# Paged scoring: POOL's scaling and subtraction of the scores issued behind the low half of the next group, and the high products first in the first pair

## The chip, the cores and the metric

The kernel runs on one core of one Trainium2 chip. The metric is the device time of one execution in microseconds (us). A difference of 0.2% (3.7 us) is about what a measurement of this kernel can tell from none.

## The reference, cut to what matters

The reference is one layer of a decoder for two groups of requests: a prompt of 1024 tokens, and 8 sample requests of 4 tokens each, whose past of 4096 tokens lies in a paged cache. The change touches the attention of the sample requests over this cache:

```python
def one(args):                                  # for each of the 8 requests
    pages, q1, c1, pe1 = args
    c_all = jnp.concatenate([pool_ckv[pages].reshape(PAST_LEN, KV_LORA), c1], axis=0)
    pe_all = jnp.concatenate([pool_kpe[pages].reshape(PAST_LEN, QK_ROPE), pe1], axis=0)
    k, v = mla_keys_values(c_all, pe_all, k_pos, w_uk, w_uv, g_qk_k)   # k is RMS-normalised per head
    return masked_attend(q1, k, v, q_pos, k_pos)                       # softmax(q k / sqrt(96)) v
```

For each of 32 pages of 128 tokens the kernel needs the scores of 8 heads x 4 queries, and for each token and head the squared length of its key, by which the scores are scaled before the softmax.

## The kernel before, in words

The program runs through a projection, the prompt's attention, the stage on the pages, the memory's keys and values, the output projection, the memory attention and the FFN. On the page stage, `phase2b` writes the order out by hand: 128 steps n, one for each pair of pages, 16 steps for one request (called batch b here); `at(n, pos, f)` puts a piece of work at a position of a step, and `run` issues it there. The order in which PE (TensorE), ACT (ScalarE), DVE (VectorE) and POOL (GpSimd) get their instructions is the order of issue (`manual_schedule`), up to step 128. SP's queue of loads in that stretch, and the compute engines behind it, are ordered by a scheduler.

Two steps share a quad of four pages:

- `quad_load` loads it transposed (`cT`) and plain (`ck`), three quads ahead. `quad_prep`, at an even step n, lets ACT round `cT` into the high part `ch` (L1362, two instructions, one for each half k of the 256 latent dimensions); at position (n+1, -2) it issues the low part `cl = cT - ch` (L1366): half k=0 on POOL, half k=1 on DVE. PE uses them from step n+2 on. `quad_rot` (L1351 to L1353) gives POOL three operations on the rope keys of two quads ahead, at the end of each odd step.
- `pair_score` is PE's work of a step. For each of two pages e it multiplies the page (stationary) with a 288-column and a 256-column piece of the weights and queries, each product split into three: high x high, high x low, low x high, for k=0 and then k=1. `mm3` (L185) issues these six in a row, so the third product of a group needs POOL's half of `cl` and the sixth DVE's. ACT squares what comes out (L1403, L1406), DVE adds the scores to `S` (L1405) and sums the squares into `ss` (L1409).

When the first 24 pages of a batch are scored, `batch_softmax` begins its pieces r: DVE turns `ss` into reciprocal roots (r 0 to 2); POOL scales 24 pages of `S` by them (r=3, L1427, at step 14 of the batch, position 3); DVE takes the maximum (r=4, L1430, at 15, position 0); the last 8 pages follow (r 5 to 8); PE, DVE and ACT bring the maximum to all partitions (r 9 to 11: ACT's copy `bc`, L1469); POOL subtracts it from `S` (L1470, also in r=11, at step 20, position 2); ACT takes the exponential (r=12, L1472, at 21, position 3). Then `quad_pv` (L1481) multiplies the weights with the values, `batch_out` (L1489 to L1499) copies and divides, `batch_close` (L1505, L1506) folds. Since the next batch is being scored meanwhile, POOL has these two operations between its `cl` halves.

Behind step 128 the generator `mem_kv` takes the keys and values of the memory: ACT makes `mh` (L204) and DVE `ml` (L207) out of the memory in eight pieces, PE multiplies them (L1549) into a PSUM tile `b` with two buffers, ACT reads each as `kr` and `sq` (L1555, L1557). The last steps of the page stage and the pieces of the last batch's softmax are issued between its parts.

Of the kernel before, what the change touches and what calls it, by code (L numbers as in the profile page):

```python
# [9 lines left out]
ALU = mybir.AluOpType  # L10
# [3 lines left out]
P = 128  # L14
NP_, NS, NT = 1024, 32, 1056
NB, ND = 8, 4
# [138 lines left out]
class Net:  # L155
# [987 lines left out]
    def phase2b(self):  # L1143
        nc, tc, I = self.nc, self.tc, self.I
        pa = self.pa3 = self.open("p3a", side="right")
        pt, px, p = self.open("p3t"), self.open("mx"), self.open("p3")
        self.mx0 = [self.t(px, [P, 8, 384], FR, f"mx0{x}") for x in "hl"]
        wk0 = [self.t(px, [P, 8, P], FR, f"wk0{x}") for x in "hl"]
        ppt, pp = self.open("ps3t", space=PSUM), self.open("ps3", space=PSUM)
# [13 lines left out]
        last = NB * 16  # L1163
        st, ev, late = {}, {}, []

        def at(n, pos, f, *a):
            ev.setdefault((n, pos), []).append(lambda: f(*a))
# [27 lines left out]
        for b in range(NB):  # L1195
            n = b * 16
            at(n - 10, 0, lambda b: st.__setitem__(b, self.batch_open(p, b)), b)
            at(n - 8, 2, lambda b: self.batch_enter(st[b], b), b)
            for r, (k, pos) in enumerate(((12, 0), (13, 0), (14, 0), (14, 3), (15, 0), (16, 0), (17, 0), (17, 3), (18, 2), (19, 2), (20, 0), (20, 2), (21, 3))):
                f = lambda b=b, r=r: self.batch_softmax(p, ppt, st[b], r, b == NB - 1)  # L1200
                if n + k <= last:
                    at(n + k, pos, f)
                else:
                    late.append(f)
            n += 16 + LAG + 15
            tail = (
                lambda b=b: self.batch_out(pt, st[b], 0),
                lambda b=b: self.batch_out(pt, st[b], 1, ppt, b == NB - 1),
                lambda b=b: self.batch_close(pt, ppt, b, st.pop(b)),
            )  # L1210
            for k, pos, f in ((0, 3, tail[0]), (2, 2, tail[1]), (3 if b == NB - 2 else 4, 3, tail[2])):
                if b < NB - 1:
                    at(n + k, pos, f)
# [48 lines left out]
        with tc.manual_schedule(engines={E.SP}):  # L1262
            self.close("ps3")
            for x in ("p3a", "p3c", "sq", "sm"):
                self.close(x)
            self.wr = self.open("wr", bufs=3, side="right")
            self.wp = self.open("w", bufs=3, side="right")
            mem = self.mem_kv(raws, wk0)
            for f in late[:3]:
                f()  # L1270
            for _ in range(6):
                next(mem)
            steps(last + 1, last + 7)
            for f in late[3:]:
                f()
            for _ in range(6):
                next(mem)
            steps(last + 7, last + 16 + LAG)
            for _ in mem:
                pass  # L1280
# [105 lines left out]
    def pair_score(self, p, pp, n, d, s, rope):  # L1386
        nc = self.nc
        b, g0 = n // 16, n % 16 * 2
        off, sc = (0, 0) if b % 2 == 0 else (32, 256)
        n0 = 32 - off  # L1390

        ps = self.t(pp, [P, 2, 512], F32, "s", 2)
        pt = self.t(pp, [P, 512], F32, "s2", 2)
        k2 = [[[d[x][:, k, g0 % 4 + e].rearrange("p j t -> p (j t)") for x in "hl"] for k in range(2)] for e in range(2)]
        w = lambda a, z: [(self.w2h[:, k, a:z], self.w2l[:, k, a:z]) for k in range(2)]
        if rope:
            rope = self.quad_rope(ps[:, 0, 320:448], *rope)
        for e in range(2):
            self.mm3(ps[:, e, :288], k2[e], w(off, off + 288))
        for e in range(2):  # L1400
            self.mm3(pt[:, e * 256 : e * 256 + 256], k2[e], w(320, 576))
        sq = self.t(p, [P, 2, 2, 256], F32, "sq", 2)
        nc.scalar.activation(sq[:, 0], ps[:, :, n0 : n0 + 256], AF.Square)  # L1403
        S = s["S"][:, g0 : g0 + 2]
        nc.vector.tensor_tensor(S, ps[:, :, sc : sc + 32], S, ALU.add)  # L1405
        nc.scalar.activation(sq[:, 1], pt.rearrange("p (e d) -> p e d", e=2), AF.Square)  # L1406
        if rope:
            yield rope
        yield lambda: nc.vector.tensor_reduce(  # L1409
            s["ss"][:, g0 : g0 + 2].rearrange("p e (z h) -> p z e h", z=2), sq.rearrange("p z e (h d) -> p z e h d", h=4), AX.X, ALU.add  # L1410
        )

    def batch_softmax(self, p, pp, s, r, final):

        nc = self.nc
        S, ss = s["S"], s["ss"]

        def norms(g0, g1, e=nc.vector):
            x = ss[:, g0:g1]
            e.tensor_tensor(x, x, s["kss"][:, g0:g1].unsqueeze(2).broadcast_to([P, g1 - g0, 8]), ALU.add)  # L1420
            sf = x.rearrange("p g h -> p (g h)")
            return self.rsqrt_steps(p, sf, sf, 1.0 / 96, e)

        def scale(e, g0, g1):
            n = (g1 - g0) * 8
            x = S[:, g0:g1].rearrange("p g (h t) -> p (g h) t", h=8)
            e.tensor_tensor(x, x, ss[:, g0:g1].rearrange("p g h -> p (g h)").unsqueeze(2).broadcast_to([P, n, 4]), ALU.mult)  # L1427

        def peak(z, g0, g1):
            nc.vector.tensor_reduce(s["m"][:, z], S[:, g0:g1].rearrange("p g m -> p m g"), AX.X, ALU.max)  # L1430

        if r == 0:
            s["it"] = norms(0, 24)
            next(s["it"])
        elif r == 1:
            next(s["it"])
        elif r == 2:
            for _ in s["it"]:
                pass
        elif r == 3:  # L1440
            scale(nc.gpsimd, 0, 24)
        elif r == 4:
            s["m"] = self.t(p, [P, 2, 32], F32, "mx", 2)
            peak(0, 0, 24)
        elif r == 5:
            s["it"] = norms(24, 32, nc.gpsimd if final else nc.vector)
            next(s["it"])
        elif r == 6:
            next(s["it"])
        elif r == 7:  # L1450
            for _ in s["it"]:
                pass
        elif r == 8:
            scale(nc.vector, 24, 32)
            peak(1, 24, 33)
            nc.vector.tensor_tensor(s["m"][:, 0], s["m"][:, 0], s["m"][:, 1], ALU.max)
        elif r == 9:
            tp = s["tp"] = self.t(pp, [P, 512], F32, "m", 1)
            nc.tensor.transpose(tp[:32, :P], s["m"][:, 0], self.ident)
        elif r == 10:  # L1460
            mm = self.t(p, [32, 1], F32, "mm", 2)
            nc.vector.tensor_reduce(mm, s["tp"][:32, :P], AX.X, ALU.max)
            s["dg"] = self.t(p, [32, 32], F32, "dg", 2)
            nc.vector.tensor_scalar(s["dg"], self.ident[:32, :32], mm, None, ALU.mult)
        elif r == 11:
            bc = self.t(pp, [P, 512], F32, "m", 1)[:, :32]
            self.spread = nc.tensor.matmul(bc, self.ones[:32], s["dg"], start=True, stop=True)
            s["bc"] = self.t(p, [P, 32], F32, "bc", 2)
            nc.scalar.copy(s["bc"], bc)  # L1469
            (nc.vector if final else nc.gpsimd).tensor_tensor(S, S, s["bc"].unsqueeze(1).broadcast_to([P, 33, 32]), ALU.subtract)  # L1470
        else:
            self.exp = nc.scalar.activation(S, S, AF.Exp, scale=SCALE)  # L1472

    def quad_pv(self, pp, Q, d, s):

        nc, S, q = self.nc, s["S"], Q % 8
        if q == 0:
            s["o"] = self.t(pp, [P, 512], F32, "o", 1)[:, :257]
            nc.tensor.matmul(s["o"][:32], S[:, 32], self.cn[:, :257], start=True, stop=False)
        for j in (1, 2, 3, 0):  # L1480
            nc.tensor.matmul(  # L1481
                s["o"][j * 32 : j * 32 + 32], S[:, q * 4 + j], d["ck"][:, j, :257], start=q == 0 and j > 0, stop=q == 7
            )
# [973 lines left out]
```

## Time and profile before

| | |
|---|---|
| Median of 3 runs | 1832.22 us (1831.4 to 1832.39) |
| The profiled execution, its own time | 1835.1 us |
| Its span, first to last instruction | 1833.4 us |
| Mean granted TensorE clock | 0.996 |
| Page stage, 400 to 858 us of the span: PE busy | 451.71 of 458 us |
| same stretch: DVE, ACT, POOL busy | 337.00, 267.50, 212.84 us |

Rows of the timeline read: start in the span, duration (of a group, if it ends in x2 or more: from the first start to the last end), engine, line, operation, output tile <- input tiles, size, count, and in brackets the idle time before it with what ended it. PE's records are longer than the distance between two starts, as products overlap; where PE is dense, the start-to-start distance is the cost of a product.

### The profile page before, as it was taken

What the parts mean: (1) busy time and instruction counts of PE and PEld (TensorE: products, weight loads), DVE (VectorE), ACT (ScalarE), POOL (GpSimd) and SP (SyncE); (2) the same over time, 40 slices, a digit from 0 to 9 for tenths busy, and PEclk for the clock granted to TensorE, in tenths of its full rate; (3) what the DMA queues carried; (4) which work ended last, traced back from release to release, by engine and by line L of the source; (5) the groups of instructions that cost most, each with busy time, mean ns of one, the idle gap of its engine ahead of it and who ended that gap; (6) DMA issues with size and microseconds to landing.
All of it is one profiled execution on the core that took longest, in us unless ns stands there. A gap on an engine that the chain in (4) does not pass through costs nothing.

```text
span 1833.4 us, 39288 instructions
## 1 busy us (share of the span) xinstructions
PE 1806.0 (99%) x14226; PEld 1702.6 (93%) x14226; DVE 1352.0 (74%) x2807; ACT 921.9 (50%) x1910; POOL 695.7 (38%) x845
## 2 busy tenths in 40 slices
PE   9999999999999999999999999999999999999999
PEld 8999777769999999998899979999999999999999
DVE  7854767757778766787645666998888888888664
ACT  7435676766655555556433556533333333444442
POOL 1021555624445444453033110377667776400000
PEclk9999999999999999999999999999999999999999
DMA  8102363558866666654555156222222222495242
GB/s 321 47 19 72 104 196 116 162 186 237 220 179 192 193 177 186 181 169 138 174 168 185 49 180 188 81 82 76 96 75 71 81 72 82 143 332 163 79 153 77
DMA packets 153187, 261.18 MB, mean 142 GB/s; under 512 B 20897, under 2 KB 97538, under 8 KB 152994
## 3 DMA queue, kind: packets, MB, share of 16 engines
q1 hardware_dynamic: 152130, 257.63, 45.4%
q8 instruction: 112, 1.84, 0.4%
q10 hardware_dynamic: 864, 1.05, 0.2%
q14 instruction: 81, 0.66, 0.1%
HBM read 212.79 MB, written 45.82 MB: 141 GB/s over the span
## 4 chain that ended last, share of the span: by engine, by line
PE 73%; issue 4%; DVE 4%; DMA 2%; SPq 2%; ACT 2%; POOL 1%; DVEq 0%; POOLq 0%; ACTq 0%
PE s L185 15%; PE d L185 12%; PE b L185 8%; PE F L185 7%; PE X L185 7%; PE E L185 7%; PE A L185 3%; PE y L185 3%; PE o L1012 2%; PE tp L997 1%; DMA ck<-ck 1%; PE o L1481 1%; DMA cT<-cT 1%; SPq L1334 1%; PE tp L185 1%
## 5 line engine op out<-in xcount | busy, mean ns | idle before, releaser
L185 PE MATMUL s<-w2h,ch 128*128 128x288 f32 (+1 forms) x1024 | 303.7, 297 | 0.5 <-ACT S L1384 0.5
L185 PE MATMUL s<-w2h,cl 128*128 128x288 f32 (+1 forms) x1024 | 295.9, 289 | 4.4 <-POOL cl L1366 3.4
L185 PE MATMUL s<-w2l,ch 128*128 128x288 f32 (+1 forms) x1024 | 294.6, 288 | 0.0
L185 PEld LDWEIGHTS s<-w2h,ch 128*128 128x128 f32 x1024 | 192.6, 188 | 8.9 <-ACT sq L1406 2.5
L185 PEld LDWEIGHTS s<-w2h,cl 128*128 128x128 f32 x1024 | 192.4, 188 | 6.5 <-POOL cl L1366 5.3
L185 PEld LDWEIGHTS s<-w2l,ch 128*128 128x128 f32 x1024 | 192.8, 188 | 0.0
L1409 DVE TENSOR_REDUCE ss<-sq 128x16 f32<-128x1024 f32 x128 | 155.3, 1213 | 32.4 <-ACT sq L1406 32.0
L1366 POOL TENSOR_TENSOR cl<-cT,ch 128x512 fp32r<-128x512 f32 x64 | 83.3, 1302 | 134.8 <-ACT ch L1362 110.0
L1406 ACT ACTIVATE sq<-s 128x512 f32<-128x512 f32 x128 | 76.5, 598 | 88.1 <-PE s L185 88.1
L1403 ACT ACTIVATE sq<-s 128x512 f32<-128x512 f32 x128 | 76.7, 599 | 74.7 <-PE s L185 72.4
L200 ACT CAST a<-brb 128x528 fp32r<-128x528 f32 x77 | 48.8, 634 | 111.0 <-PE d L185 105.0
L185 PE MATMUL d<-a,w 128*128 128x264 f32 x768 | 95.2, 284 | 0.0
L201 DVE TENSOR_TENSOR a<-brb,a 128x528 fp32r<-128x528 f32 x77 | 54.2, 705 | 54.8 <-ACT a L200 54.7
L185 PEld LDWEIGHTS d<-a,w 128*128 128x128 f32 x768 | 94.3, 188 | 0.0
L2093 POOL TENSOR_TENSOR lo<-s,hi 128x1024 fp32r<-128x1024 f32 x20 | 63.8, 3188 | 45.7 <-ACT hi L2092 45.7
L185 PE MATMUL mm<-wlo,xh 128*128 128x256 f32 (+3 forms) x272 | 77.0, 286 | 0.1
L185 PE MATMUL mm<-whi,xh 128*128 128x256 f32 (+3 forms) x272 | 77.0, 285 | 0.0
L185 PE MATMUL mm<-whi,xl 128*128 128x256 f32 (+3 forms) x272 | 76.9, 287 | 0.0
L2148 ACT COPY a<-A 128x264 f32<-128x264 f32 x43 | 16.1, 375 | 120.6 <-PE A L185 113.2
L1362 ACT CAST ch<-cT 128x512 fp32r<-128x512 f32 x128 | 73.4, 626 | 0.2 <-issue 0.2
L2214 POOL TENSOR_TENSOR cv<-cv,row 128x1056 f32<-128x1056 f32 x22 | 65.1, 2959 | 21.0 <-ACT cv L2213 21.0
L185 PE MATMUL d<-a,hi 128*128 128x264 f32 x552 | 72.0, 284 | 0.0
(745 smaller groups left out, 6341.2 us busy)
## 6 DMA issues: line engine op xcount, KB each, us to landing
cT<-cT SPq DMA_DIRECT2D x256, 160.0 KB, 2.9
ck<-ck SPq DMA_DIRECT2D x256, 144.0 KB, 3.5
raw<-w_up SPq DMA_DIRECT2D x44, 512.0 KB, 3.6
wsumd<-wsum SPq DMA_DIRECT2D x26, 512.0 KB, 3.8
actd<-cv SPq DMA_DIRECT2D x44, 264.0 KB, 2.3
brb<-actd SPq DMA_DIRECT2D x44, 264.0 KB, 5.6
wsum<-w_down SPq DMA_DIRECT2D x22, 512.0 KB, 3.7
raw<-wsumd SPq DMA_DIRECT2D x20, 512.0 KB, 3.7
```

The source lines that it names most:

```text
L185: x = self.nc.tensor.matmul(out, l, r, start=first and i == 0, stop=last and i == len(seq) - 1)
L200: first = {"act": nc.scalar.copy, "pool": nc.gpsimd.tensor_copy, "dve": nc.vector.tensor_copy}[eng](hi, src)
L201: low = lambda: nc.vector.tensor_tensor(lo, src, hi, ALU.subtract)
L997: nc.tensor.transpose(tp[:, z * P : z * P + P], u[e][:, j * P : j * P + P], self.ident)
L1012: nc.tensor.matmul(u["o"][g : g + 64, o : o + m * P], s["v"][:, j, h % 4], th[:, z * P : (z + m) * P], start=j == 0, stop=b == len(banks) - 1,
L1362: nc.scalar.copy(d["h"][:, k], src[k])
L1366: (nc.vector if k else nc.gpsimd).tensor_tensor(d["l"][:, k], src[k], d["h"][:, k], ALU.subtract)
L1403: nc.scalar.activation(sq[:, 0], ps[:, :, n0 : n0 + 256], AF.Square)
L1406: nc.scalar.activation(sq[:, 1], pt.rearrange("p (e d) -> p e d", e=2), AF.Square)
L1409: yield lambda: nc.vector.tensor_reduce(s["ss"][:, g0 : g0 + 2].rearrange("p e (z h) -> p z e h", z=2), sq.rearrange("p z e (h d) -> p z e ...
L2093: eng.tensor_tensor(lo, src, hi, ALU.subtract)
L2214: nc.gpsimd.tensor_tensor(cv, cv, row, ALU.mult)
```

## The change

Four edits:

1. In batches 0 to 6 the order of two pieces changes. POOL's scaling (r=3) moves from (14, 3) to (15, 0), and so behind the low half that is issued at (15, -2); the maximum (r=4) moves with it, from (15, 0) to (15, 3). Batch 7 keeps its positions.
2. POOL's subtraction leaves r=11 and becomes a piece of its own, r=13, at (21, 0), behind the low half at (21, -2). The exponential stays at (21, 3). In batch 7 DVE subtracts in r=11 as before.
3. In step 0, `pair_score` issues the four high products of three of its four groups first, then their two low products each; the fourth group is as before.
4. Behind step 128, the steps 129 to 131 (the products of batch 6 with the values, and the copy of their result) are issued after the first part of `mem_kv` and not after the sixth.

```diff
@@ -1196,12 +1196,14 @@
-            for r, (k, pos) in enumerate(((12, 0), (13, 0), (14, 0), (14, 3), (15, 0), (16, 0), (17, 0), (17, 3), (18, 2), (19, 2), (20, 0), (20, 2), (21, 3))):
+            for r, (k, pos) in enumerate(((12, 0), (13, 0), (14, 0), (14, 3) if b == NB - 1 else (15, 0), (15, 0) if b == NB - 1 else (15, 3), (16, 0), (17, 0), (17, 3), (18, 2), (19, 2), (20, 0), (20, 2), (21, 3))):
                 f = lambda b=b, r=r: self.batch_softmax(p, ppt, st[b], r, b == NB - 1)
...
+            if b < NB - 1:
+                at(n + 21, 0, lambda b=b: self.batch_softmax(p, ppt, st[b], 13, False))
@@ -1268,9 +1270,11 @@
             for f in late[:3]:
                 f()
-            for _ in range(6):
+            next(mem)
+            steps(last + 1, last + 4)
+            for _ in range(5):
                 next(mem)
-            steps(last + 1, last + 7)
+            steps(last + 4, last + 7)
@@ -1395,10 +1399,18 @@
-        for e in range(2):
-            self.mm3(ps[:, e, :288], k2[e], w(off, off + 288))
-        for e in range(2):
-            self.mm3(pt[:, e * 256 : e * 256 + 256], k2[e], w(320, 576))
+        jobs = [(ps[:, e, :288], k2[e], w(off, off + 288)) for e in range(2)]
+        jobs += [(pt[:, e * 256 : e * 256 + 256], k2[e], w(320, 576)) for e in range(2)]
+        if n:
+            for j in jobs:
+                self.mm3(*j)
+        else:
+            for low in range(2):
+                for o, a, c in jobs[:3]:
+                    for k in range(2):
+                        for i in range(1 if low else 2):
+                            nc.tensor.matmul(o, a[k][low], c[k][i], start=low + k + i == 0, stop=low + k == 2)
+            self.mm3(*jobs[3])
@@ -1467,9 +1479,16 @@
-            (nc.vector if final else nc.gpsimd).tensor_tensor(S, S, s["bc"].unsqueeze(1).broadcast_to([P, 33, 32]), ALU.subtract)
+            if final:
+                self.less(nc.vector, s)
+        elif r == 13:
+            self.less(nc.gpsimd, s)
...
+    def less(self, e, s):
+        S = s["S"]
+        e.tensor_tensor(S, S, s["bc"].unsqueeze(1).broadcast_to([P, 33, 32]), ALU.subtract)
```

POOL's queue at the end of batch 1's scoring, before the change; `S` with `ss` is the scaling and `S` with `bc` the subtraction, the rest belongs to the quads of the batch that follows:

```order
L1427 TENSOR_TENSOR S_6048<-S_6048,ss_6049 128x768
L1366 TENSOR_TENSOR cl_7731<-cT_7440,ch_7730 128x512
...
L1245 MEMSET ck_6483 128x4
L1470 TENSOR_TENSOR S_6048<-S_6048,bc_8192 128x1056
L1366 TENSOR_TENSOR cl_8157<-cT_7855,ch_8156 128x512
L1351 TENSOR_TENSOR krq_8201<-cT_7997,cosT_5030 128x128
```

And after it, at the same place of the queue:

```order
L1370 TENSOR_TENSOR cl_7731<-cT_7440,ch_7730 128x512
L1439 TENSOR_TENSOR S_6048<-S_6048,ss_6049 128x768
...
L1247 MEMSET ck_6483 128x4
L1370 TENSOR_TENSOR cl_8157<-cT_7855,ch_8156 128x512
L1491 TENSOR_TENSOR S_6048<-S_6048,bc_8192 128x1056
L1355 TENSOR_TENSOR krq_8201<-cT_7997,cosT_5030 128x128
```

In both pairs the low half and the operation on `S` have changed places; nothing else of the queue has, there and at the same two places of the other batches up to 6.

PE's queue at step 0, before: the first page's group `s` of 288 columns, where `cl` is the low part (with buffer numbers: `ch_1103` and `cl_1104` are the first quad).

```order
L1381 MATMUL s_1108_5744<-bd_829_4477,krq_1101_5723 128x128
L185 MATMUL s_1111_5751<-w2h_206_1705,ch_1103_5728 128x288
L185 MATMUL s_1111_5751<-w2l_207_1706,ch_1103_5728 128x288
L185 MATMUL s_1111_5751<-w2h_206_1705,cl_1104_5729 128x288
L185 MATMUL s_1111_5751<-w2h_206_1705,ch_1103_5728 128x288
```

After, from the seventh product of the same step on:

```order
L1412 MATMUL s_1111_5751<-w2h_206_1705,ch_1103_5728 128x288
L1412 MATMUL s_1111_5751<-w2l_207_1706,ch_1103_5728 128x288
L1412 MATMUL s2_1112_5752<-w2h_206_1705,ch_1103_5728 128x256
...
L1412 MATMUL s2_1112_5752<-w2l_207_1706,ch_1103_5728 128x256
L1412 MATMUL s_1111_5751<-w2h_206_1705,cl_1104_5729 128x288 x4
L1412 MATMUL s2_1112_5752<-w2h_206_1705,cl_1104_5729 128x256 x2
```

The first product with `cl` stood third and now stands thirteenth, behind the twelve high products of three groups.

ACT's queue behind step 128, before: `oo` is the copy of batch 6's products with the values, which PE writes into `o`.

```order
L204 ACTIVATE mh_14383<-ck_14160,cols_58 128x256 x4
L204 ACTIVATE mh_14383<-ck_14250,cols_58 128x256 x4
L1489 COPY oo_14442<-o_13932 128x257
L200 CAST hi_14465<-ck_14334 128x1024
L200 CAST hi_14500<-raw_14498 128x1024
```

And after:

```order
L204 ACTIVATE mh_14383<-ck_14160,cols_58 128x256
L1508 COPY oo_14397<-o_13932 128x257
L204 ACTIVATE mh_14383<-ck_14160,cols_58 128x256 x3
L204 ACTIVATE mh_14383<-ck_14250,cols_58 128x256 x4
L200 CAST hi_14465<-ck_14334 128x1024
```

The copy `oo` has moved ahead of seven of the eight `mh`. On DVE, the reciprocal L1495 and the division L1499 of batch 6 have moved up too, to behind the first and the third of the eight `ml`; on PE the two kinds of product of L1493 and L1505 have moved up among those with `mh`.

## The prediction

> **What bounds the kernel now.** I read the page's first part, then PE's waits, then PE's timeline at each wait of the page stage, and last the other engines' timelines around it. The first part says which engine sets the time:
>
> ```profile
> PE 1806.0 (99%) x14226; PEld 1702.6 (93%) x14226; DVE 1352.0 (74%) x2807; ACT 921.9 (50%) x1910; POOL 695.7 (38%) x845
> ```
>
> PE is the bound everywhere, and none of its products is removed. So the change can gain only what PE waits, and POOL's 38% do not matter as a total, only by when `cl` is ready. The waits of PE that the edits touch, by total us, times and longest:
>
> ```profile
> PE s L185 <- POOL cl L1366: 3.4, 8, 1.1
> ...
> PE s L185 <- DVE cl L1366: 1.0, 1, 1.0
> ```
>
> Eight waits for POOL's half of the low part, one for DVE's: small against 1833 us, 0.24% together. What the table counts as idle is less than what a wait costs, though, as one of the eight shows on PE's timeline (batch 1, step 22):
>
> ```profile
> 534.18 0.38 PE L185 MATMUL s<-w2h,ch 128*128 128x288 f32 x1
> 534.40 0.29 PE L185 MATMUL s<-w2l,ch 128*128 128x288 f32 x1
> 534.96 0.40 PE L185 MATMUL s<-w2h,cl 128*128 128x288 f32 x1 [0.27 <-POOL cl L1366]
> 535.20 0.30 PE L185 MATMUL s<-w2h,ch 128*128 128x288 f32 x1
> 535.33 0.29 PE L185 MATMUL s<-w2l,ch 128*128 128x288 f32 x1
> ```
>
> Undisturbed starts are 0.13 apart (535.20 to 535.33). Here 0.56 and then 0.24 pass, so the wait costs 0.43 + 0.11 = 0.54, that is 0.27 more than the 0.27 in the brackets: the record before it covers 0.16, and the product behind it starts 0.11 late.
>
> **The subtraction (seven moves).** ACT and POOL around that wait:
>
> ```profile
> 527.69 1.15 ACT L1362 CAST ch<-cT 128x512 fp32r<-128x512 f32 x2
> ...
> 530.95 0.18 ACT L1469 COPY bc<-m 128x32 f32<-128x32 f32 x1
> ...
> 534.74 1.08 ACT L1472 ACTIVATE S<-S 128x1056 f32<-128x1056 f32 x1
> ```
>
> ```profile
> 531.20 2.46 POOL L1470 TENSOR_TENSOR S<-S,bc 128x1056 f32<-128x1056 f32 x1 [7.01 <-ACT bc L1469]
> 533.61 1.29 POOL L1366 TENSOR_TENSOR cl<-cT,ch 128x512 fp32r<-128x512 f32 x1
> ```
>
> POOL idles 7 us for `bc`, subtracts, and only then makes the `cl` whose input ACT had finished long before: the first of the two casts ends about half way through its 1.15, at 528.3. Put first, `cl` runs in POOL's idle time from about 528.4 to 529.7. PE wants it at 534.53 (534.40 + 0.13), so 4.8 us of slack replace a lateness of 0.43. The subtraction starts when `bc` is there, at 531.20 as before, since `cl` ends 1.5 earlier; it ends at 533.66, and the exponential at 534.74 keeps its place. What comes behind it on POOL, the three rope operations of the step, starts 1.25 earlier than now. The move adds no instruction; the DMAs of the quads (SP's queue) are issued three quads ahead and PE waits for none of them.
>
> **The scaling (seven moves).** Only batch 0 shows a wait here. ACT's cast, POOL's two operations and PE:
>
> ```profile
> 451.98 1.14 ACT L1362 CAST ch<-cT 128x512 fp32r<-128x512 f32 x2
> ```
>
> ```profile
> 454.44 2.08 POOL L1427 TENSOR_TENSOR S<-S,ss 128x768 f32<-128x768 f32 x1 [7.00 <-DVE ss L246]
> 456.49 1.27 POOL L1366 TENSOR_TENSOR cl<-cT,ch 128x512 fp32r<-128x512 f32 x1
> ```
>
> ```profile
> 457.81 0.40 PE L185 MATMUL s<-w2h,cl 128*128 128x288 f32 x1 [1.11 <-POOL cl L1366]
> ```
>
> After the move `cl` runs from 452.6 to 453.9, and the scaling still starts at about 454.5, when `ss` is ready. The maximum on DVE reads what POOL scaled; it is now queued behind one `kss` and one addition to `S` and not ahead of them. DVE's sum stays the same, and the addition, which frees the PSUM tile and lets ACT copy, comes earlier. So this cover is not at risk, and I cost it at nothing.
>
> Both moves together: all eight waits go. Cost now: 3.4 + 8 x 0.27 = 5.6 us; taken as -5.5. Bounds: -5.6 if nothing is late behind them, and -3.4 if only the idle time of the table comes back.
>
> **The first pair.** PE at step 0, and DVE's half of the low part:
>
> ```profile
> 402.94 0.38 PE L185 MATMUL s<-w2h,ch 128*128 128x288 f32 x1
> ...
> 403.56 0.29 PE L185 MATMUL s<-w2l,ch 128*128 128x288 f32 x1
> 404.88 0.40 PE L185 MATMUL s<-w2h,cl 128*128 128x288 f32 x1 [1.02 <-DVE cl L1366]
> ```
>
> ```profile
> 404.14 0.68 DVE L1366 TENSOR_TENSOR cl<-cT,ch 128x512 fp32r<-128x512 f32 x1
> ```
>
> DVE's half is written at 404.82, and PE's sixth product waits for it until 404.88. DVE's queue up to there is unchanged, so that time stands. With twelve high products first, and the low one of k=0 behind them (POOL's half is ready, as the third product does not wait now), PE has issued 13 and not 5 products by about 404.7, and waits some 0.2. Eight products more are done at 404.88: four of 288 columns at 0.13 and four of 256 at 0.12, together 1.0. So -1.0; at most 1.3 (1.19 late plus 0.11 behind), and 0 if the next pair's work, whose squares on ACT come no earlier, holds PE back again. I stay near the upper end because PE's next steps have two PSUM buffers.
>
> **Behind step 128.** Here an edit can cost. ACT, then PE, then DVE, before:
>
> ```profile
> 855.83 3.29 ACT L204 ACTIVATE mh<-ck,cols 128x256 fp32r<-128x256 f32 x8
> 859.02 0.36 ACT L1489 COPY oo<-o 128x257 f32<-128x257 f32 x1
> 859.28 1.06 ACT L200 CAST hi<-ck 128x1024 fp32r<-128x1024 f32 x1
> ...
> 862.12 2.02 ACT L1560 ACTIVATE ck<-ck 128x1024 f32<-128x1024 f32 x2
> 864.34 0.37 ACT L1555 COPY kr<-b 128x256 f32<-128x256 f32 x1 [0.20 <-PE b L1549]
> 864.60 0.39 ACT L1557 ACTIVATE sq<-b 128x256 f32<-128x256 f32 x1
> ```
>
> ```profile
> 855.23 1.94 PE L1481 MATMUL o<-ck,S 128*32 128x257 f32 x32
> 857.99 0.36 PE L1549 MATMUL b<-mh,wk0h 128*128 128x256 f32 x1 [0.82 <-ACT mh L204]
> ```
>
> ```profile
> 857.63 0.22 DVE L1405 TENSOR_TENSOR S<-s,S 128x64 f32<-128x64 f32 x1
> ```
>
> ```profile
> 865.20 0.53 PE L1505 MATMUL m<-fold,oo 128*128 128x32 f32 x4
> 865.56 0.37 PE L1549 MATMUL b<-mh,hi 128*128 128x256 f32 x1
> ```
>
> The 0.82 at 857.99 is put down to `mh`, but its first piece was done at about 856.3; the instruction also waits for DVE, whose last addition to `S` ends at 857.85 in a PSUM tile whose space `b` takes over. That stays. New is that ACT does one `mh`, then waits in order for `oo`, whose input ends at 857.17 (855.23 + 1.94). The seven other `mh` queue behind it: they start at 857.24 + 0.26 = 857.5 and not at 856.23, one every 0.40 ((859.02 - 855.83) / 8), and the cast `hi` starts at 860.3 and not at 859.28. ACT is 1.0 late. PE has DVE's `ml` to wait for in that stretch anyway; ACT's delay reaches it at the third group of products, 865.56, which needs the first of two buffers `b` read by `kr` and `sq`. ACT comes to them after the casts, the squares and the `olT` copy at about 865.3 (864.14, where the squares end now, + 1.0 + 0.15, my estimate for `olT`, a quarter of the columns of `oo`, which held ACT for 0.26), ends at 865.95, and PE goes on at 866.0: +0.4. Against that, the fold of batch 6 leaves PE's dense part (0.36 between 865.20 and 865.56) for its waits. Taken +0.4; bounds -0.4 and +1.5 (all of ACT's 1.0, and half as much again, a guess, for the two small operations moved into DVE's `ml`).
>
> Sum: -5.5 - 1.0 + 0.4 = -6.1. The profiled execution took 1835.1 (span 1833.4 and 1.7 around it) and would take 1829.0; it stands 2.9 over the median of the runs, and I carry the difference over: 1832.2 - 6.1 = **1826.1 us**. By the bounds its own range is -7.3 to -3.9 (the lower ends of the gains not all at once), 1824.9 to 1828.3.
>
> **The clock, which shifts with the work.** Two stretches of equal kind in the windows view (busy times by engine, then the granted clock of PE):
>
> ```profile
> 879.60:886.50 6.90, 6.90 (x20) 5.64 (x21) 4.65 (x19) 1.51 (x2) 0.00 (x0) 0.51 0.30 96
> ```
>
> ```profile
> 893.10:896.60 3.50, 2.48 (x16) 1.84 (x15) 3.04 (x10) 3.22 (x7) 0.00 (x0) 1.00 0.77 220
> ```
>
> For 6.9 us behind a run of tiny products PE had half its clock, in the second stretch, where it idled 1 of 3.5 us, it had all. Half the clock for 6.9 us costs at most 3.4; I take 3, since waits in it don't scale. All the work there moves 6 us forward, so whether such a stretch is punished can change, either way. [...]
>
> **The rivals.**
>
> 1. *A drop of the clock goes.* The one at 879.60 is not repeated: 1826.1 - 3 = 1823.1 us. For: the shift of 6 us; against: a run of tiny products remains in the same order. Chance 0.17.
> 2. *Given back.* A drop appears behind another thin stretch (893.10 idles as much), or the tail costs 3 rather than 0.4 because ACT's lateness is met at each group of `mem_kv`: 1826.1 + 3 = 1829.1 us, within 0.2% of before. Chance 0.18.
> 3. *The waits are not removed*, because something else ends last right behind `cl` (DVE's half, the rope operand): only the first pair's 1.0 is left, 1831 to 1832. Against it stands DVE's half for step 22:
>
> ```profile
> 529.93 0.69 DVE L1366 TENSOR_TENSOR cl<-cT,ch 128x512 fp32r<-128x512 f32 x1
> ```
>
> It is written at 530.6, and PE starts the step at 534.18. Chance 0.03.
> 4. *Slower: POOL's waits change places.* POOL works in order; if the cast of `ch` comes so late that `cl` ends after `bc` is ready, the subtraction, the exponential and, behind it on ACT, the next quad's cast are late by up to one `cl`. It decides from 1.5 us of delay of ACT (529.7 against 531.2), and costs up to 1.29 for each of seven batches, 9.0 us, with the old waits still there: about 1840 us. ACT idles before most of its work on this stage, so chance 0.05.
>
> **How the numbers follow.** The forecast itself has 0.57. The range holds the time 8 times in 10: from 1823.0 (the forecast and most of rival 1) to 1829.6 (most of rival 2). Faster by over 0.2% (below 1828.6): forecast 0.56, rival 1 0.17, a little of rival 2 0.03, together 0.76. Within 0.2%: 0.01 + 0.15 + 0.03 = 0.19. Slower: 0.05. 0.2%, 3.7 us, is about what can be told from no change.
>
> **What would show it.** Right: PE's waits name POOL's `cl` no more, or for under 0.5 us; in step 22 of batch 1 POOL has `cl` some 3 us ahead of the subtraction, which starts just after `bc`; PE's wait in step 0 is about 0.2 and falls on a low product; the page stage is 6 us shorter and the stretch behind step 128 up to 1 us longer, with ACT's `oo` after one `mh`. Wrong: another releaser takes POOL's place in PE's waits; ACT waits for POOL's subtraction before the exponential; the stretch of `mem_kv` grows by 3 us or more; the drop of the clock at 879.60 is gone or has company, which moves the time by 3 us with the page stage as forecast.

## The result and the profile after

| | before | changed |
|---|---|---|
| median of 14 runs | 1831.81 us (1829.56 to 1834.74) | 1828.57 us (1826.23 to 1831.22) |
| ratio | | 0.9979, 95% interval 0.9972 to 0.9986 |
| the profiled execution, its span | 1833.4 us | 1826.0 us |

By the ratio the changed kernel is faster by 0.21%, 3.9 us (the two medians alone differ by 3.2); the forecast was 6.1. The ratio's interval is 0.07% to either side, so a change of 0.2% can be told from none here. The profiled executions differ by 7.4 us, which is more than the change is worth. To see what it is worth I cut PE's time at products that both kernels have: the rope product of step 0, the first product of batch 6 with the values behind step 127, the first product that sums squares in the memory's keys and values, and the first product with a diagonal (L1602, L1621) behind it. The "page stage" lies between the first two, the "tail" between the second and the third. In the changed kernel the first three lie at 401.39, 848.89 and 862.43 us, in before at 402.80, 855.23 and 868.47.

| us | before | changed | difference |
|---|---|---|---|
| up to the page stage (same work in both) | 402.80 | 401.39 | -1.41 |
| page stage | 452.43 | 447.50 | -4.93 |
| tail | 13.24 | 13.54 | +0.30 |
| from there to the first diagonal | 24.57 | 23.23 | -1.34 |
| from there to PE's last product | 936.23 | 936.19 | -0.04 |

The first row and the fourth are mostly the clock's: before had half of it for 6.83 us in each, the changed kernel for none and for 3.41 (against that, in the first row, the changed kernel has a wait of 1.40 for DVE at 243 us that before has not). What the change itself does is in the second and third row, and 0.3 us of it, as e5 will show, in the fourth. In PE's waits POOL's `cl` has gone, and on the stretch of the edits four waits are new:

```profile
PE m L1479 <- DVE dg L1476: 1.0, 1, 1.0
...
PE m L1524 <- DVE oo L1518: 0.4, 1, 0.4
...
PE b L1568 <- ACT sq L1576: 0.3, 1, 0.3
...
PE s L1385 <- ACT S L1388: 0.3, 1, 0.3
```

The first and the last lie in the page stage, the other two in the tail.

Batch 1, step 22, is as forecast. ACT's `bc`, POOL's two operations, PE:

```profile
527.95 0.18 ACT L1481 COPY bc<-m 128x32 f32<-128x32 f32 x1
...
531.74 1.08 ACT L1487 ACTIVATE S<-S 128x1056 f32<-128x1056 f32 x1
```

```profile
525.41 1.30 POOL L1370 TENSOR_TENSOR cl<-cT,ch 128x512 fp32r<-128x512 f32 x1 [4.30 <-ACT ch L1366]
528.21 2.46 POOL L1491 TENSOR_TENSOR S<-S,bc 128x1056 f32<-128x1056 f32 x1 [1.50 <-ACT bc L1481]
```

```profile
531.40 0.30 PE L185 MATMUL s<-w2l,ch 128*128 128x288 f32 x1
531.54 0.29 PE L185 MATMUL s<-w2h,cl 128*128 128x288 f32 x1
531.67 0.29 PE L185 MATMUL s<-w2h,ch 128*128 128x288 f32 x1
```

POOL has `cl` 4.8 us before PE wants it and still starts the subtraction 0.08 us behind `bc`; the starts on PE are 0.13 to 0.14 apart, where 0.56 and 0.24 had passed.

Step 0 is as forecast too: the high products run on, and the six low ones take 1.04 us (403.16 to 404.20), 0.28 more than undisturbed (4 x 0.13 + 2 x 0.12), as they meet DVE's half, written at 403.41.

```profile
403.04 0.28 PE L1412 MATMUL s<-w2l,ch 128*128 128x256 f32 x1
403.16 1.21 PE L1412 MATMUL s<-w2h,cl 128*128 128x288 f32 x6
404.20 0.28 PE L185 MATMUL s<-w2h,ch 128*128 128x256 f32 x1
```

```profile
402.73 0.68 DVE L1370 TENSOR_TENSOR cl<-cT,ch 128x512 fp32r<-128x512 f32 x1
```

**Where the missing part went.** Setting the starts of PE's steps in the two traces beside each other, each old wait gives what it cost (1.38, 0.82, 0.54, 0.60, 0.54, 0.59, 0.55, 0.57: together 5.59), the first pair 1.00, and then two places of batch 0 take 0.43 and 1.18 back. (Where a wait is given below by what it costs, it is such a difference of starts, and the time in brackets of a row is less.) These are PE's rows there, each after the last product that ran undisturbed:

```profile
463.43 0.28 PE L185 MATMUL s<-w2h,cl 128*128 128x256 f32 x1
463.98 0.46 PE L1385 MATMUL s<-bd,krq 128*128 128x128 f32 x2 [0.27 <-ACT S L1388]
...
470.28 0.28 PE L185 MATMUL s<-w2h,cl 128*128 128x256 f32 x1
471.58 0.40 PE L1479 MATMUL m<-dg,ones 32*128 32x32 f32 x2 [1.02 <-DVE dg L1476]
```

The first is put down to ACT, which copies the rope scores, but ACT itself had waited 2.22 us for DVE's addition; both waits are DVE's. DVE's and POOL's rows of the changed kernel at the two operations that are late:

```profile
450.44 1.36 DVE L241 SCALAR_TENSOR_TENSOR rqa<-rqy 128x192 f32<-128x192 f32 x1
...
470.38 0.27 DVE L1474 TENSOR_REDUCE mm<-m 32x1 f32<-32x128 f32 x1
470.68 0.85 DVE L1476 TENSOR_SCALAR dg<-ident,mm 32x32 f32<-32x32 f32 x1
```

```profile
450.29 1.29 POOL L1370 TENSOR_TENSOR cl<-cT,ch 128x512 fp32r<-128x512 f32 x1 [5.24 <-ACT ch L1366]
...
470.22 1.27 POOL L1370 TENSOR_TENSOR cl<-cT,ch 128x512 fp32r<-128x512 f32 x1 [2.85 <-ACT ch L1366]
```

In the trace of before the same two operations on DVE:

```profile
452.83 0.35 DVE L241 SCALAR_TENSOR_TENSOR rqa<-rqy 128x192 f32<-128x192 f32 x1
...
472.99 0.23 DVE L1464 TENSOR_SCALAR dg<-ident,mm 32x32 f32<-32x32 f32 x1
```

An operation of the reciprocal root (L241; called the root's step below) takes 1.36 and not 0.35, the diagonal 0.85 and not 0.23: 1.01 + 0.62 = 1.63 us. Each runs beside one of the two low halves that the change moved into POOL's idle time, and ends just behind it (POOL at 451.58, DVE at 451.80; POOL at 471.49, DVE at 471.53). And DVE has no reserve there, before or after, as the windows over this stretch say (before, then changed; behind the length come the busy time and count of PE, of PE's weight loads, of DVE, ACT and POOL, then the clock, DMA's share and its GB/s):

```profile
445.00:473.00 28.00, 26.67 (x213) 26.22 (x213) 27.23 (x59) 15.06 (x34) 12.43 (x18) 1.00 0.85 240
```

```profile
445.00:473.00 28.00, 26.71 (x212) 26.28 (x211) 27.35 (x57) 15.00 (x33) 12.17 (x17) 1.00 0.86 242
```

DVE is busy for 27.2 of 28 us, PE for 26.7. In batch 0 DVE also makes four copies that the later batches do not have.

The later batches show that such stretching need not cost PE anything. In batches 1 to 6 as well, the root's step or the operation behind it takes 1.10 to 1.37 beside POOL's low half, and PE has no wait there. In batch 1 of the changed kernel:

```profile
505.10 1.36 DVE L241 SCALAR_TENSOR_TENSOR rqa<-rqy 128x192 f32<-128x192 f32 x1
```

```profile
504.95 1.29 POOL L1370 TENSOR_TENSOR cl<-cT,ch 128x512 fp32r<-128x512 f32 x1 [4.64 <-ACT ch L1366]
```

Nor was the kernel before free of it: there DVE's addition of `kss` ran beside a low half and took 1.10 to 1.12 in batches 0 to 6, where it takes 0.36 to 0.44 now. So the scaling's move exchanged one such meeting for another. In before, batch 0:

```profile
459.69 1.12 DVE L1420 TENSOR_TENSOR ss<-ss,kss 128x64 f32<-128x64 f32 x1
```

So the theory: in batch 0 DVE has no time to spare, and the two low halves, put beside DVE's operations, stretch these by what PE then waits. The rival: the new waits have to do with one edit alone, or with the first pair's earlier start.

### The profile page after: what moved, and what is told of

Read it like the earlier page. It is cut to its first block, busy times and chain, and to the rows that moved or that the text cites. A ratio compares the mean times of both kernels' runs of the same rounds, so it can differ in the third digit from the quotient of the medians.

```text
span 1826.0 us, 39295 instructions
## 1 busy us (share of the span) xinstructions
PE 1799.3 (99%) x14226; PEld 1698.7 (93%) x14226; DVE 1355.1 (74%) x2807; ACT 921.5 (50%) x1910; POOL 697.5 (38%) x845
## 4 chain that ended last, share of the span: by engine, by line
PE 78%; DVE 5%; ACT 2%; issue 1%; SPq 1%; POOL 1%; DMA 1%; DVEq 0%; ACTq 0%; POOLq 0%
PE s L185 20%; PE d L185 12%; PE b L185 8%; PE F L185 7%; PE X L185 7%; PE E L185 7%; PE A L185 3%; PE y L185 3%; PE o L1012 2%; PE o L1500 2%; PE tp L997 1%; PE tp L185 1%; PE s L1385 1%; PE tp L950 1%; ACT pr L989 1%
## 5 line engine op out<-in xcount | busy, mean ns | idle before, releaser
L185 PE MATMUL s<-w2h,ch 128*128 128x256 f32 x1018 | 301.9, 297 | 0.5 <-ACT S L1388 0.5
L185 PE MATMUL s<-w2h,cl 128*128 128x256 f32 x1018 | 293.2, 288 | 0.0
L185 PE MATMUL s<-w2l,ch 128*128 128x256 f32 x1018 | 292.9, 288 | 0.0
```

The costliest lines, as they stand in the source:

```text
L185: x = self.nc.tensor.matmul(out, l, r, start=first and i == 0, stop=last and i == len(seq) - 1)
```

## The experiments

The page stage, the tail and the stretch behind it come from one profile each; where the clock halves for 3.41 us behind the tail, that stretch is 1.5 us longer. The ratio is to the kernel before, with its 95% interval.

| kernel | page stage | tail | to the diagonal (half clock) | median | ratio |
|---|---|---|---|---|---|
| before | 452.43 | 13.24 | 24.57 (6.83) | 1831.81 | |
| changed | 447.50 | 13.54 | 23.23 (3.41) | 1828.57 | 0.9979 (0.9972 to 0.9986) |
| e1, POOL's moves only | 448.47 | 13.26 | 22.97 (3.41) | 1829.57 | 0.9986 (0.9977 to 0.9995) |
| e2, scaling back | 447.42 | 13.54 | 23.26 (3.41) | 1828.47 | 0.9984 (0.9975 to 0.9993) |
| e3, subtraction back | 450.93 | 13.58 | 23.23 (3.41) | 1832.25 | 0.9998 (0.9989 to 1.0007) |
| e4, copies on ACT | 446.20 | 13.54 | 21.75 (0) | 1826.17 | 0.9966 (0.9952 to 0.9979) |
| e5, tail back | 447.68 | 13.24 | 21.44 (0) | 1826.84 | 0.9973 (0.9964 to 0.9982) |
| e6, e4 and e5 | 446.04 | 13.31 | 21.37 (0) | 1825.30 | 0.9962 (0.9948 to 0.9975) |
| e7, two low halves on DVE | 447.69 | 13.54 | 23.32 (3.41) | 1829.10 | 0.9985 (0.9976 to 0.9994) |
| e8, no diagonal | 446.63 | 13.61 | 21.68 (0) | 1827.40 | 0.9973 (0.9963 to 0.9984) |
| e9, e6 and e8 | 445.48 | 13.25 | 21.40 (0) | 1826.00 | 0.9970 (0.9961 to 0.9979) |
| e10, changed again | 447.42 | 13.54 | 23.27 (3.41) | 1829.13 | 0.9982 (0.9972 to 0.9992) |

**e1: POOL's two moves alone.**

```diff
-        if n:
+        if n >= 0:
...
-            next(mem)
-            steps(last + 1, last + 4)
-            for _ in range(5):
+            for _ in range(6):
                 next(mem)
-            steps(last + 4, last + 7)
+            steps(last + 1, last + 7)
```

> The moves of POOL's scaling and subtraction alone; the first pair and the stretch behind step 128 are as before. I measure the page stage from the rope product of step 0 to the first product of batch 6's last steps with the values: 452.43 us before (402.80 to 855.23), 447.50 in the changed kernel (401.39 to 848.89); and the tail from there to the first product that sums squares: 13.24 before, 13.54 changed. Theory A (DVE is the pace of batch 0: without POOL's waits, PE meets DVE's lateness, 0.43 + 1.18 us): the eight waits are gone, the two new ones are there, whether the first pair is faster or not; page stage 448.5, tail 13.24, the whole 4.0 us under before. Rival B (the new waits come from the first pair's earlier start, which ran into DVE's queue): no new waits, page stage 446.9, the whole 5.6 under before.

448.47 and 13.26: theory A, and not B, and the runs agree (0.9 to 4.2 us under before, where B needs 5.6). The two new waits are there at their full size without the edit of the first pair:

```profile
468.71 0.35 PE L1383 MATMUL s<-bd,krq 128*128 128x128 f32 x1 [0.27 <-ACT S L1386]
...
476.32 0.29 PE L1477 MATMUL m<-dg,ones 32*128 32x32 f32 x1 [1.02 <-DVE dg L1474]
```

**e2: the scaling back**, in all batches (part of one line):

```diff
-... (14, 3) if b == NB - 1 else (15, 0), (15, 0) if b == NB - 1 else (15, 3), ...
+... (14, 3), (15, 0), ...
```

> The changed kernel, with the scaling and the maximum at their old places in all batches. Theory A (DVE is the pace of batch 0, the scaling's move gained nothing but another name for the wait): POOL's wait of 1.38 us in batch 0 returns, and the two new waits of 0.43 and 1.18 shrink to 0.4 or less together, since DVE has that time to catch up; page stage 447.1 to 447.7, against 447.50 with the move; in batches 1 to 6 no wait appears, as there was none of the scaling before. Rival C (the new waits belong to the subtraction's move and POOL's low half beside DVE's small operations, whatever the scaling does): they stay at 1.6 and the 1.38 comes on top, page stage 448.9.

447.42, as A: the moves of scaling and maximum, fourteen of them, are worth nothing (447.50 with them). The old wait is back; of the new ones, that of 0.43 is gone and 0.26 is left at the diagonal. The root's step takes 0.35 again. The diagonal still takes 0.87 beside POOL's low half, so that meeting belongs to the subtraction's move, and it costs PE little here, where the old wait has held PE back. DVE and POOL, then PE:

```profile
451.13 0.35 DVE L241 SCALAR_TENSOR_TENSOR rqa<-rqy 128x192 f32<-128x192 f32 x1
...
471.30 0.87 DVE L1476 TENSOR_SCALAR dg<-ident,mm 32x32 f32<-32x32 f32 x1
```

```profile
452.74 2.08 POOL L1439 TENSOR_TENSOR S<-S,ss 128x768 f32<-128x768 f32 x1 [6.99 <-DVE ss L246]
454.77 1.28 POOL L1370 TENSOR_TENSOR cl<-cT,ch 128x512 fp32r<-128x512 f32 x1
```

```profile
456.11 0.40 PE L185 MATMUL s<-w2h,cl 128*128 128x288 f32 x1 [1.10 <-POOL cl L1370]
```

**e3: the subtraction back.**

```diff
-            if b < NB - 1:
-                at(n + 21, 0, lambda b=b: self.batch_softmax(p, ppt, st[b], 13, False))
...
-            if final:
-                self.less(nc.vector, s)
-        elif r == 13:
-            self.less(nc.gpsimd, s)
+            self.less(nc.vector if final else nc.gpsimd, s)
```

> The changed kernel, with the subtraction at its old place in all batches. Both theories of the prediction's kind say that six waits of 0.54 to 0.60 us return, one in each of batches 1 to 6. Theory A: the two new waits of batch 0 lie ahead of the subtraction and stay (0.43 and 1.18), and the 0.82 behind it returns: page stage 447.5 + 3.4 + 0.8 = 451.7, which is 0.7 under before. Rival C (the new waits belong to the subtraction's move): they go, page stage 450.1.

450.93 lies between the two, and both had a part wrong. The six waits of the later batches and the one of batch 0 came back. But of the new waits, which A held to stay, the one for the diagonal shrank from 1.18 to 0.61 (and the other from 0.43 to 0.16): with the subtraction ahead of it, POOL's low half no longer runs beside the diagonal, which takes 0.23 again, while the root's step still takes 1.35. So each of the two moves brought its own collision: the scaling's the one at the root, the subtraction's the one at the diagonal.

```profile
471.70 0.23 DVE L1474 TENSOR_SCALAR dg<-ident,mm 32x32 f32<-32x32 f32 x1
```

```profile
471.98 0.29 PE L1477 MATMUL m<-dg,ones 32*128 32x32 f32 x1 [0.42 <-DVE dg L1474]
```

**e4: the four copies on ACT.** In this generator `first` is 2 for the copies in question and 0 elsewhere.

```diff
-            nc.vector.tensor_copy(hl[:, :, i % 2 * tn : i % 2 * tn + tn], tp)
+            (nc.scalar.copy if first else nc.vector.tensor_copy)(hl[:, :, i % 2 * tn : i % 2 * tn + tn], tp)
```

> The changed kernel, but the four copies of transposed blocks out of PSUM in steps 11 to 17 (0.68 us each, 128x512) are made by ACT and not by DVE. Nothing else differs on the page stage. Theory A: DVE is 2 us earlier by the end of step 17, more than its lateness, and both new waits go: page stage 447.5 - 1.6 = 445.9. If ACT then is late in its turn, its copies show in PE's waits and the page stage stays at about 447.5. Rival C (a wait on one collision of POOL's low half with DVE's small operation just ahead of PE's product, not DVE's load): the wait of 1.18 stays at 0.6 or more, page stage 446.9.

446.20, between A and C. The wait of 0.43 went, and with it one of 0.42 at PE's transposes, at 446 us, that before had too; the wait for the diagonal is 0.75. DVE's load and the collision both count: with DVE earlier, the diagonal still stretches beside the low half, and PE still comes ahead of it.

```profile
472.94 0.86 DVE L1476 TENSOR_SCALAR dg<-ident,mm 32x32 f32<-32x32 f32 x1
```

```profile
473.85 0.40 PE L1479 MATMUL m<-dg,ones 32*128 32x32 f32 x2 [0.68 <-DVE dg L1476]
```

**e5: the tail back**, by the lower part of e1's diff.

> The changed kernel, with the steps 129 to 131 issued after the sixth part of the memory's keys and values, as before. Theory A (the earlier issue costs what ACT's seven late pieces and the small products add): page stage as changed, 447.5, tail 13.24 in place of 13.54, the whole 0.3 us under the changed kernel. Rival D (the earlier issue gains, since the fold leaves PE's dense part): tail 13.9, the whole 0.4 over the changed kernel. The runs' interval will not tell 0.3 us; the profile's stretch does.

13.24, as A, and 21.44 to the diagonal. Among the profiles without a drop of the clock in that stretch the kernels with the edit behind step 128 need 21.75 and 21.68 there, those without it 21.37 to 21.44. So that edit costs 0.3 in the tail and 0.3 behind it, 0.6 together.

**e6: the copies on ACT and the tail back.**

> The changed kernel with both: the four copies of steps 11 to 17 on ACT, and the tail as before. Theory A: page stage 445.9, tail 13.24, the whole 1.9 us under the changed kernel, ratio to before 0.9970. If the copies only move the lateness to ACT: page stage 447.5, ratio to before 0.9978.

446.04 and 13.31, as A: the copies on ACT bring no new wait of PE. The ratio, 0.9962, is the lowest of all.

**e7: two low halves on DVE.** The two that collided, both in batch 0.

```diff
+                    quads[Q + 1]["Q"] = Q + 1
                     at(n + 1, -2, self.quad_prep(quads[Q + 1]))
...
-                (nc.vector if k else nc.gpsimd).tensor_tensor(d["l"][:, k], src[k], d["h"][:, k], ALU.subtract)
+                (nc.vector if k or d["Q"] in (8, 11) else nc.gpsimd).tensor_tensor(d["l"][:, k], src[k], d["h"][:, k], ALU.subtract)
```

> The changed kernel, but in two steps of batch 0's softmax (the low parts issued at steps 15 and 21, those that POOL computed beside DVE's root operation of 1.36 us and beside its diagonal of 0.85 us) DVE makes both halves of the low part, and POOL none. DVE gets two operations of 0.68 us more; POOL no longer runs beside the two. Theory E (the new waits are made of the two operations that stretched beside POOL's low half, 1.0 + 0.6 us): the root operation takes 0.36, the diagonal 0.23, the waits of 0.43 and 1.18 shrink to 0.3 or less together at these places, page stage 446.2. Rival F (DVE's mere load, the stretching has another cause): DVE is later by 0.68 at the first place, the waits grow to 2.3, page stage 448.2.

447.69, neither. The durations are theory E's: the root's step 0.35, the diagonal 0.23, and the wait for the diagonal shrank to 0.35. But a new collision took their place: DVE's two low halves, at step 15, took 2.66 together and not 1.3, since the second began during POOL's scaling and ended 0.55 behind it (which ends at 454.92). PE lost 0.28 right behind that low half, 0.35 at the start of a step (461.88), and the wait at 463.98 of the changed kernel grew from 0.43 to 0.83.

```profile
451.23 0.35 DVE L241 SCALAR_TENSOR_TENSOR rqa<-rqy 128x192 f32<-128x192 f32 x1
...
452.81 2.66 DVE L1371 TENSOR_TENSOR cl<-cT,ch 128x512 fp32r<-128x512 f32 x2
...
472.33 0.23 DVE L1477 TENSOR_SCALAR dg<-ident,mm 32x32 f32<-32x32 f32 x1
```

```profile
452.84 2.08 POOL L1440 TENSOR_TENSOR S<-S,ss 128x768 f32<-128x768 f32 x1 [6.99 <-DMA ck<-ck]
```

```profile
464.88 0.28 PE L185 MATMUL s<-w2h,cl 128*128 128x256 f32 x1
465.84 0.46 PE L1386 MATMUL s<-bd,krq 128*128 128x128 f32 x2 [0.67 <-ACT S L1389]
```

**e8: no diagonal.**

```diff
-            s["dg"] = self.t(p, [32, 32], F32, "dg", 2)
-            nc.vector.tensor_scalar(s["dg"], self.ident[:32, :32], mm, None, ALU.mult)
+            s["mm"] = mm
...
-            self.spread = nc.tensor.matmul(bc, self.ones[:32], s["dg"], start=True, stop=True)
+            self.spread = nc.tensor.matmul(bc, s["mm"].broadcast_to([32, P]), self.ident[:32, :32], start=True, stop=True)
```

> The changed kernel, but PE spreads the maximum without DVE's diagonal: the maxima of 32 rows, read with a stride of zero, are the stationary operand and the identity the moving one. In batch 0 DVE then has no operation between the maximum and PE's product that can stretch beside POOL's low half (0.85 us, where it takes 0.23 alone). Theory E (the wait of 1.18 is that stretching and the 0.5 that DVE is late): the maxima are written at 470.65 in the changed kernel's time, PE wants them at 470.40, so the wait falls to 0.3 to 0.5, page stage 446.7 to 446.9, against 447.50. Rival F (DVE's mere load): the lateness only moves on to the next thing that PE waits for, page stage 447.3 or more.

446.63, as E: 0.87 less than the changed kernel. Of the wait of 1.18 some 0.3 is left (473.66, which is 473.54 + 0.12, to 473.96), and is what the maxima themselves are late (written at 473.91):

```profile
473.64 0.27 DVE L1474 TENSOR_REDUCE mm<-m 32x1 f32<-32x128 f32 x1
```

```profile
473.54 0.28 PE L185 MATMUL s<-w2h,cl 128*128 128x256 f32 x1
473.96 0.40 PE L1478 MATMUL m<-ident,mm 32*128 32x32 f32 x2
```

**e9: copies on ACT, no diagonal, tail back.**

> All three: the four copies of steps 11 to 17 on ACT, no diagonal, and the tail as before. With the copies alone the page stage was 446.20 and the wait for the diagonal 0.75; without a diagonal DVE's maxima are there as PE comes to them. Theory E: page stage 445.5, tail 13.24, the whole 0.5 us under the kernel with copies and tail; ratio to before 0.9960. Rival F: page stage 446.0 as without this edit.

445.48 and 13.25, as E. Nothing of batch 0 waits any more; by the stages it is the fastest kernel, 2.3 us under the changed one in page stage and tail together (458.73 against 461.04). Its runs, ratio 0.9970, cannot be told from those of e6 at 0.9962, and they had less of the clock: the mean granted clock of its ten runs is 0.9978, that of e6's five 0.9992.

**e10: the changed kernel again.**

> The changed kernel once more, in the same call as the two others, as a measure of scatter. If the drops of the clock belong to the kernel, this profile has the one of 3.41 us at 875, and the page stage starts at 401.4; if they fall by chance, the start lies anywhere between 401.4 and 405.2 and the drops at 217 to 262 and at 875 to 886 come and go. Page stage 447.5, tail 13.54; ratio to before 0.9972 to 0.9986.

The same kernel has its drops at other places: this profile has them at 290.6 and 877.7, the first profile had one at 875.1 alone. The page stage starts at 404.61 and not at 401.39, and page stage and tail are the same to 0.1 us. So the drop ahead of the page stage comes and goes in one and the same kernel; the one behind the tail is in both profiles, and whether it falls by chance too is not shown.

## Why the prediction was right, and where it was off

- **The eight waits:** taken at 5.5, 5.59 measured. That a wait costs 0.27 more than its brackets show held at each.
- **The subtraction:** right in its own terms. The low half is ready 4.8 us early, the subtraction follows `bc`, the exponential has moved by the same 3.0 us (534.74 to 531.74) as PE's products ahead of the old wait.
- **The first pair:** 1.0 forecast, 1.00 measured, with 0.28 of the wait left where 0.2 was expected.
- **The scaling, the step that failed:** "this cover is not at risk, and I cost it at nothing". I looked at which operations changed places on DVE, and not at what the low half would run beside once it had moved. In batch 0 one low half ran beside the root's step and, by the subtraction's move, another beside the diagonal: +1.61 us, by which nearly all of the gap to the forecast goes (-6.1 + 1.6 = -4.5). The subtraction's working has the same gap: it looked at POOL and ACT alone. e2 shows that the scaling's moves are worth nothing, e2 and e3 that the second collision is the subtraction's, e8 and e9 that without the diagonal and with DVE relieved the whole 1.6 comes back. The prediction had asked what would be late next on POOL and on ACT, and of DVE only for its half of one step in batch 1; batch 0, where DVE is busy for 27.23 of 28 us, it had not looked at.
- **Behind step 128:** +0.4 forecast, +0.30 measured in the tail and +0.3 behind it, 0.6 in all, inside the bounds. The old wait of 0.82 was read rightly: it is still there with 0.74, now under the name of DVE's addition to `S`. The place was right: ACT does one `mh`, waits 0.91 for `oo`'s input, and is late with the `sq` that frees `b` for the third group, which by the forecast had to start at about 859.6 in the changed kernel's time (866.0 - 6.4) and started at 859.51:

```profile
850.90 0.38 ACT L1508 COPY oo<-o 128x257 f32<-128x257 f32 x1 [0.91 <-PE o L1500]
...
859.08 0.38 ACT L1576 ACTIVATE sq<-b 128x256 f32<-128x256 f32 x1
```

```profile
854.23 0.63 PE L1524 MATMUL m<-fold,oo 128*128 128x32 f32 x4 [0.40 <-DVE oo L1518]
...
859.51 0.39 PE L1568 MATMUL b<-mh,hi 128*128 128x256 f32 x1 [0.34 <-ACT sq L1576]
```

  Not foreseen was the wait at 854.23: DVE's division `oo` stands between its `ml` pieces, and PE's fold, which has moved up, waits for it.
- **The sum:** page stage and tail give -4.93 + 0.30, with 0.3 behind the tail -4.3 us, where the runs say -3.9 (-5.1 to -2.6) and the forecast -6.1. The measured median, 1828.57, lies in the range given (1823.0 to 1829.6), but just outside the one that the sum's own bounds gave (1824.9 to 1828.3), and -3.9 is the very end of their -7.3 to -3.9. The room that holds it was left for the second rival, whose mechanism did not occur; that much is luck.
- **The rivals:** the time came out near that of the second, "given back" (1829.1), but by another mechanism; that the clock or the tail would do it was wrong. The first, a drop of the clock that goes, is not shown to be the change's doing: the drop at 879 was 6.83 us long in the one profile of before and 3.41 in both of the changed kernel, but between none and 3.41 in kernels that differ from it in a copy or two, and the runs gained no more than page stage and tail explain. That the drops follow the place of the work in time, for which this rival counted the shift of 6 us, was an assumption of mine that no run shows: in e10 the same kernel, with nothing moved, has a drop ahead of the page stage that its first profile has not. The granted clock on record with the runs speaks against it too: its mean is 0.9983 in the 23 runs of the changed kernel (e10's with them) and 0.9987 in the 69 of before that were taken beside the experiments, and at equal clock the changed kernel is faster all the same (at 0.999, 1827.7 in 8 runs against 1831.4 in 20; at 0.998, 1829.6 in 11 against 1832.9 in 17). The third and the fourth did not occur.

What stays open: how the 1.6 us split between DVE's load and the two collisions, which act together: the diagonal's costs 0.3 or less where PE comes to it later (e2), and the root's costs nothing in batches 1 to 6. e4 (load off, diagonal still stretched) and e8 (diagonal off, load still there) each give back a half or more (1.30, of which 0.42 is an older wait, and 0.87); the root's collision alone was not taken out without another wait coming in (e2, e7).

## What to carry to other kernels

When an operation of POOL is moved into POOL's idle time, look at what DVE does in that very stretch: a windows row over it for DVE's load, and DVE's timeline for operations that would run beside it (in batch 0 two of them took 1.36 and 0.85 us there, and 0.35 and 0.23 before). An edit that removes PE's wait for one engine gains only down to the next engine's lateness: in batch 0, with DVE busy for 27.2 of 28 us, taking away the wait for POOL's scaling gained nothing (447.50 against 447.42), and taking load off DVE did (446.20). Effects of a few microseconds are told apart by cutting the traces at products that both kernels have, sooner than by the medians.

## What the runs showed of the hardware

- Some of DVE's operations on SBUF tiles, begun while an operation of POOL was running, ended shortly behind it, however long they take elsewhere. In seven batches of the changed kernel the root's step or the operation behind it took 1.10 to 1.37 (0.35 and 0.36 without POOL beside them), and each ended 0.21 or 0.22 behind POOL's low half. The addition of `kss` ended 0.07 to 0.09 behind POOL's operation, in before (1.10 to 1.12) as in the changed kernel (0.36 to 0.44). The diagonal of 32x32 took 0.85 instead of 0.23 and ended 0.04 behind. In e7 a low half took 2.06 instead of 0.68 beside POOL's scaling of 2.08 and ended 0.55 behind. DVE's reductions of `sq` (1.20 to 1.22), the one for the maxima (0.27) and its addition out of PSUM (0.20 to 0.23) kept their times beside operations of POOL in the changed kernel. What sets the two kinds apart, no run shows.
- The clock's drops, to half, lasted 3.41 us in the changed kernel's profile (875.12 to 878.53) and 6.83 us, twice as long, in that of before (217.52 to 224.35 and 879.62 to 886.45). Behind the tail a drop of 3.41 us cost 1.5 us (23.2 against 21.7). Of the twelve profiles of before, changed and the ten experiments, one has a drop of 6.83 us there, six have one of 3.41 and five have none. Between 217 and 291 us the half clock lasts from nothing (changed) to 6.83 us (before). What sets a drop off, no run shows: in the changed kernel PE was busy for all of the 3.41 us ahead of it (871.71 to 875.12). A row of the changed kernel inside its drop, with a clock of 0.50 and PE busy for all of it:

```profile
875.20:878.50 3.30, 3.30 (x9) 2.52 (x8) 2.08 (x13) 1.08 (x1) 0.00 (x0) 0.50 0.46 122
```

- The page stage starts between 401.39 and 405.16 us in these profiles, with the same work of the compute engines ahead of it in all of them. That scatter alone is as much as the change is worth.
